# Attention row blocks 4 to 7 copied by ScalarE's DMAs and transposed as fp32r, with two exponentials issued earlier

## The chip, the cores and the metric

The kernel runs on one core of a Trainium2 chip. The metric is the device time of one execution in microseconds, the median over several runs. TensorE (PE) multiplies into PSUM and loads its stationary operand by separate instructions (PEld in the profile); VectorE (DVE), ScalarE (ACT) and GpSimd (POOL) do the element-wise work; DMAs are issued by SyncE (SP) or, as in this change, by ScalarE.

## The reference

One decoder block on x of shape (1024, 1024) in float32: an RMS norm, an input projection, forgetting attention with 8 heads of 64 columns beside a gated mixing path, an output projection with a residual, and a gated MLP with a short causal convolution. The change is in the attention:

```python
c = jnp.cumsum(log_f, axis=1)
...
logits = jnp.einsum('bqhd,bkhd->bhqk', qi, k).astype(jnp.float32) * scale
logits = logits + ci[..., None] - c_k
causal = pi[:, None] >= key_pos[None, :]
logits = jnp.where(causal, logits, -jnp.inf)
p = jax.nn.softmax(logits, axis=-1).astype(v.dtype)
return jnp.einsum('bhqk,bkhd->bqhd', p, v)
```

## The kernel before

Large products run in fp32r, a 4-byte type with a shortened mantissa that TensorE takes in one pass. To keep float32 accuracy each operand is split into a high part (a cast to fp32r) and a low part (the difference, again fp32r), and three products high x high, high x low, low x high are added in PSUM.

**The attention stage** (about 222 to 357 us of the span) works head by head. A head's 1024 query rows are 8 row blocks of 128; block j has (j + 1) x 128 columns because of the causal mask. For each block:

- `logits_mm` (lines 1002 to 1012) multiplies queries and keys into a PSUM tile of `place()`, of which there are two.
- `logits_min` (lines 1014 to 1035) on VectorE writes the masked logits to SBUF, into `places[h, i]`, and takes their row minimum. `places[h, i]` holds the blocks 2i and 2i + 1 side by side; its buffer is chosen by `TTAG`.
- `logits_exp` (lines 1037 to 1040) on ScalarE takes the exponential in place and adds up its rows. Each is followed by a short read of the accumulator.
- `turn_p` (lines 1057 to 1067) transposes 128 x 128 pieces of the finished blocks on TensorE, with the tile itself as the stationary operand and the identity `ident` as the moving one, four pieces to a PSUM bank; ScalarE casts the bank to the high part (line 1065) and VectorE subtracts for the low part (line 1066).
- `values` (lines 1071 to 1090) multiplies the two parts with the head's values.

**The order.** `STEPS` cuts each head into five steps of two groups of transposes (the last step has one). In head h, step s, the loop (lines 1186 to 1262) first issues `turn_p` for the groups of the following step, so the step 4 of head h turns the first two column blocks (k = 0, 1) of head h + 1, from row blocks 4, 5, 6 and 7 in that order. It then runs `values` on what the step before turned, and between the groups the logits and minima of the next head: blocks 7 and 6 in step 0, 5 and 4 in step 1, 3 and 2 in step 2, 1 and 0 in step 3. A minimum goes to the list `due`; the step after takes it over as `last` and issues its exponentials at its end. So exponentials 7 and 6 stand in step 1, 5 and 4 in step 2, 3 and 2 in step 3, 1 and 0 in step 4. TensorE's order is fixed by `seq`; on the other engines instructions are placed by a list scheduler, and `after(tc, later, earlier)` only says that one comes behind the other in the queue. `row_tail` (step 1) writes the row sums to DRAM by a DMA that ScalarE issues (line 963). In heads 0 to 5 products of the gate path (`sg_out`, lines 1104 to 1106) are put in after steps 2 and 4 as filler. The last head has no logits beside it.

Head 0's logits and exponentials come ahead of this loop. The tile tags: `t2` and `t3` have one buffer each, `H` has four, shared by early activations, by `attF` and by blocks 4 to 7 of odd heads.

Of the kernel before, what the change touches and what calls it, by code (L numbers as in the profile page):

```python
# [8 lines left out]
F32 = mybir.dt.float32  # L9
F32R = mybir.dt.float32r  # L10
# [4 lines left out]
P = 128  # L15
# [48 lines left out]
def after(tc, later, earlier):  # L64
    tc.add_manual_dep(later.ins, earlier.ins.name, mybir.DependencyInfo(
        mybir.DependencyClass.NoSync, mybir.DependencyReason.DATA), reason="order")
# [8 lines left out]
def block_kernel(ctx: ExitStack, tc: tile.TileContext, xT, xtok, wuv, wuh, wv0, wva, wvk, wvl, wqk, cpk, bfv,  # L75
                 ggain, g2r, gfr, wsp, woa, wos, wup, wdn, out):
    nc = tc.nc
    act, dve, pool, pe, sp = Line(nc.scalar, tc), Line(nc.vector, tc), Line(nc.gpsimd, tc), nc.tensor, nc.sync

    cst = ctx.enter_context(tc.tile_pool(name="cst", bufs=1))  # L80
# [12 lines left out]
    def nm(s):  # L93
        uid[0] += 1
        return f"{s}_{uid[0]}"

    BUFS = {"x1": 4, "x2": 2, "t3": 1, "t2": 1, "t01": 1, "V": 4, "H": 4, "wy": 2, "gg": 2,
            "pt": 3, "G": 4, "A": 2, "whl": 4, "raw": 4}

    LATE = ("A", "G", "whl", "pt")  # L100
# [1 line left out]
    def sb(tag, shape, dt=F32):  # L102
        return (base if tag == "x1" else raws if tag == "raw" else late if tag in LATE else early).tile(shape, dt, tag=tag, bufs=BUFS[tag], name=nm(tag))

# [27 lines left out]
        pe.matmul(wps, warm[:, 0:P], warm, start=True, stop=True)  # L132
    dve.memset(one, 1.0)
    dve.memset(lim, BIG)
    ident = cst.tile([P, P], F32, name="ident")
    make_identity(nc, ident)
    maskb = cst.tile([P, P], BF16, name="maskb")
    pool.memset(maskb, 0.0)
    pool.affine_select(out=maskb, in_=maskb, pattern=[[-1, P]], compare_op=ALU.is_ge,
# [44 lines left out]
    def xset(tags):  # L184
        r = []
        for t in tags:
            if t == "x1":
                r.append([sb(t, [P, 2, 512], F32R) for _ in range(2)])
            else:
                b = sb(t, [P, 2, 2, 512], F32R)  # L190
                r.append([b[:, 0], b[:, 1]])
        return r

    RAW = {n: [sb(t, [P, 2, 512]) for t in tags] for n, tags in (
        ("x21", ("V", "V")), ("x11", ("H", "H")), ("x22", ("x1", "x2")), ("x12", ("t3", "t2")))}
    XS = {n: xset(tags) for n, tags in (("B11", ("V", "V")), ("T2", ("H", "H")), ("B21", ("x1", "x2")))}

    def xs(n, hl, k):
        return XS[n][k // 2][hl][:, k % 2, :]

    def x2(n, hl, j):
        return XS[n][j][hl]

# [55 lines left out]
    for p_ in range(2):  # L259
        t = sb("G", [P, 2, 2, 512])  # L260
# [37 lines left out]
    for o in (slice(0, 256), slice(256, 512)):  # L298
        h, l, src = xs("B11", 0, 0)[:, o], xs("B11", 1, 0)[:, o], xr("x11", 0)[:, o]
# [86 lines left out]
    for k in range(4):  # L386
        dve.scalar_tensor_tensor(out=xr("x12", k), in0=xr("x12", k), scalar=gk(k), in1=tmp[k // 2][2][:, k % 2],
                                 op0=ALU.mult, op1=ALU.subtract)
    XS["T3"] = xset(("x1", "x2"))
    for j in range(2):  # L390
# [5 lines left out]
    for w in gb:  # L396
        dve.tensor_tensor(out=w[:, 0, :], in0=w[:, 0, :], in1=w[:, 1, :], op=ALU.add)
    XS["T1"], mid = xset(("H", "H")), sb("t3", [P, 4, 512])
    for k in range(4):
# [13 lines left out]
    for k in range(4):  # L413
        t2 = tmp[k // 2][1][:, k % 2]
# [290 lines left out]
    gg = []  # L705
# [53 lines left out]
    V, vhigh = [], []  # L759
# [21 lines left out]
    def seq(m):  # L781

        if order:
            after(tc, m, order[0])
        order[:] = [m]
# [98 lines left out]
    abs_, places = [None] * 8, {}  # L884
# [66 lines left out]
    attF = [None] * 4  # L951


    TTAG = [("gg", "gg"), ("wy", "wy"), ("t2", "H"), ("t3", "H")]
    exs = []
    def row_tail(h):

        p, hh, rs = h // 2, h % 2, rows[h]
# [38 lines left out]
    casts, los = [], []  # L997
# [16 lines left out]
    def logits_min(h, j, ps):  # L1014

        i, jj = j // 2, j % 2
        w1, w2 = (2 * i + 1) * P, (2 * i + 2) * P
        if jj == 1:
            tp = sb(TTAG[i][h % 2], [P, w1 + w2])
            places[h, i] = (tp[:, 0:w1], tp[:, w1:w1 + w2])  # L1020
        n = (j + 1) * P
        mn = sml.tile([P, 1], F32, tag="mn", name=nm("mn"))
        o, s, k = places[h, i][jj], ps[:, 0:n], msk[:, 1024 - n:1024]
        if chunk(n) < min(n, 512):
            o, k = (v.rearrange("p (b c) -> p b c", b=2) for v in (o, k))
            s = ps.rearrange("p (b c) -> p b c", b=2)[:, :, 0:chunk(n)]
        m = dve.tensor_tensor_reduce(out=o, in0=s, in1=k, scale=ss1[:, j:j + 1],
                                     scalar=lim[:, 0:1], op0=ALU.add, op1=ALU.min, accum_out=mn)
        if h and j == 5:
            after(tc, m, recips[h - 1])  # L1030
        if h and j == 3:
            after(tc, m, los[-1])
        if h == 7 and j == 0:
            after(tc, m, los[-2])
        return mn

    def logits_exp(h, j, mn):
        t = places[h, j // 2][j % 2]
# [18 lines left out]
    def turn_p(g):  # L1057

        ptr = bank()
        pt = sb("pt", [P, 2, 512], F32R)  # L1060
        for half, k, j0, c, w in spans(g):
            for j in range(j0, 4 * half + 4):
                o = c + (j - j0) * P
                seq(pe.transpose(ptr[:, o:o + P], places[g[0], j // 2][j % 2][:, k * P:(k + 1) * P], ident))  # L1064
        casts.append(act.copy(pt[:, 0, :], ptr))  # L1065
        los.append(dve.tensor_tensor(out=pt[:, 1, :], in0=ptr, in1=f32(pt[:, 0, :]), op=ALU.subtract))  # L1066
        return pt
# [86 lines left out]
    def fill(key):  # L1154
        for _ in range(FILL.get(key, 0)):
            next(filler, None)
# [27 lines left out]
    due = []  # L1184
    turned = [turn_p(g) for g in STEPS[0]]
    for n, step in enumerate(STEPS):
        h, s = n // 5, n % 5
        if s == 0 and h < 6:
            head_loads(h + 2)
        if h == 7 and s == 0:  # L1190
            for _ in filler:
                pass
            wo_load((0, 1))
            wo_load((2, 3))
        if h in (2, 4, 6) and s == 4:
            for o in (slice(0, 512), slice(512, 1024)):
                pair_half(h // 2 - 1, o)
        now, turned = turned, []
        last, due = due, []
        if n == 35:  # L1200
            psl.release()
            psl = tc.alloc_tile_pool(name="psc", bufs=4, space=bass.MemoryType.PSUM, reuse_waits="tile")
            banks8[0, 0] = lbank()
            wmm(0, 0, banks8[0, 0], (0,))
        for g in STEPS[n + 1] if n + 1 < len(STEPS) else []:
            if n == 36 and turned:
                for e in held + [mrow]:
                    after(tc, logits_exp(*e), casts[-1])
            turned.append(turn_p(g))
            if n == 36 and len(turned) == 2:  # L1210
                after(tc, casts[-1], exs[-1])
        if n == 34:
            mrow = (7, 0, logits_min(7, 0, mrow))
        if n == 33:

            held, last = last, []
        if n == 34:
            last, held = held[:1], held[1:] + last
        if n == 35:
            last, held = held[:1], held[1:]  # L1220
        if s == 1 and h % 2 == 0:
            attF[h // 2] = sb("H", [P, 2, 1024])
        if s == (1 if h < 7 else 2):
            recips[h] = dve.reciprocal(rows[h], rows[h])
        out_copy = None
        if n == 37:
            row_tail(7)
        if n in EARLY:
            wmm(0, 0, banks8[0, 0], EARLY[n])
        if n == 39:  # L1230
            banks8[4, 0] = lbank()
            wmm(4, 0, banks8[4, 0], (0,))
        for c, (g, pt, js) in enumerate(zip(step, now, NEXT[s])):
            out_copy = values(g, pt) or out_copy
            last_copy = out_copy
            if h < 7:
                for j in js:
                    if n == 33 and j == 0:
                        mrow = logits_mm(7, 0, place())
                        continue  # L1240
                    due.append((h + 1, j, logits_min(h + 1, j, logits_mm(h + 1, j, place()))))
            if s == 1 and h < 7 and c == 0:
                row_tail(h)

        for e in last:
            x = logits_exp(*e)
            after(tc, x, casts[-1] if n == 34 else out_copy or casts[-1])
        fill((h, s))
        for _ in range(min(len(SPLIT), 1 if n == 9 else 2)):
            ws_, k, wr = SPLIT.pop(0)  # L1250
            wt = sb("whl", [P, 2, 512], F32R)
            ws_[k] = wt
            after(tc, act.copy(wt[:, 0], wr), out_copy or casts[-1])
            pool.tensor_tensor(out=wt[:, 1], in0=wr, in1=f32(wt[:, 0]), op=ALU.subtract)
        if n == 2:
            vh = sb("A", [P, 2, 4, 256])
            sp.dma_start(out=vh, in_=vu.rearrange("h p m c -> p h m c"))
        if n in UPPER:
            tt = UPPER.index(n)
            low = evac_v(tt, 1, vh[:, tt // 4, tt % 4, :])  # L1260
            after(tc, low(), los[-1])
            after(tc, vhigh[0], exs[-1])
# [186 lines left out]
    for i in range(AHEAD):  # L1449
# [4 lines left out]
        if i == 0:  # L1454

            last = flip(7)
# [219 lines left out]
    for p_, n in ((upl, "B11"), (upl, "T2"), (upl, "B21"), (upl, "T3"), (upr, "T1"), (upr, "T4"), (upr, "B22")):  # L1676
        t = ut_(p_, "x" + n, [P, 2, 4, 512], F32, 1)
# [71 lines left out]
    x1, x3, u2 = ([t[:, m, :] for m in range(4)] for t in big)  # L1749
# [144 lines left out]
```

## Time and profile before

| What | Value |
|---|---|
| Time, median of 3 runs | 1044.55 us (1044.23 to 1044.55) |
| The profiled execution's own time | 1043.81 us |
| Its span (first to last instruction) | 1042.1 us |
| Granted TensorE clock, mean | 0.998 |
| Transposes of the attention, line 1064 | 288, median 272 ns of one |
| Casts of line 1065 | 72, 40.4 us busy, 584 ns |
| Subtractions of line 1066 | 72, 47.4 us busy, 686 ns |

The page counts busy time of each engine. Matmuls are pipelined: one of 272 ns may be followed by the next after less, so what they cost is read from the distance of their starts in the timeline. An entry "x8" in the timeline is a run of eight merged ones, with the time from the first start to the last end. Shapes are written "partitions x elements", `pb<-ident,t` is "written <- read", and a bracket gives the idle time of the engine and what ended it. The waits in the attention stage are few on TensorE; the longest sums belong to engines that are ahead of it:

```profile
ACT pt L1065 <- PE pb L1064: 24.4, 16, 4.6
POOL H L973 <- ACT wy L1039: 23.2, 1, 23.2
DVE pt L1066 <- ACT pt L1065: 10.1, 28, 1.2
```

The columns are who waited for whom, the total in us, the number of waits and the longest.

### The profile page before, as it was taken

Reading aid. Unit: us, or ns where it says so; the run is one execution under the profiler, and the core shown is the slowest. Engines: PE = TensorE matmul, PEld = TensorE weight load, DVE = VectorE, ACT = ScalarE, POOL = GpSimd, SP = SyncE. Lnnn points to the kernel's source line nnn. Section 1 sums busy time; section 2 is a strip of 40 time slices with the busy share of each in tenths; the row PEclk is TensorE's granted clock in tenths of the full one; section 3 lists DMA queues with packets and bytes.
Section 4 is the critical chain, followed back from the end, with each engine's and each line's share of the span. In section 5 each row is a group of like instructions: output and inputs, shape, how many; then the busy total and the mean of one; then the engine's idle time right before and its main releaser. Section 6 shows DMA issues by size and latency. Waiting matters only on the chain.

```text
span 1042.1 us, 14271 instructions
## 1 busy us (share of the span) xinstructions
PE 1034.4 (99%) x4998; PEld 869.6 (83%) x4998; DVE 892.3 (86%) x1302; ACT 564.2 (54%) x1003; POOL 221.9 (21%) x167
## 2 busy tenths in 40 slices
PE   9999999999999999999999999999999999999997
PEld 7988888988888888888888888888888888888886
DVE  6899887888888888998999998898997857997774
ACT  6776632457776857644444444444544544444654
POOL 0000232500322540343334323333331000000000
PEclk9999999999999999999999999999999999999999
DMA  9622558885645553231353432332322998333432
GB/s 340 231 82 97 153 156 250 238 256 171 203 130 172 187 169 111 81 122 60 131 178 131 139 120 71 132 101 81 122 81 91 327 330 293 110 92 101 150 115 99
DMA packets 67467, 161.66 MB, mean 155 GB/s; under 512 B 8110, under 2 KB 9254, under 8 KB 67396
## 3 DMA queue, kind: packets, MB, share of 16 engines
q1 hardware_dynamic: 67124, 160.72, 47.6%
q8 instruction: 39, 0.64, 0.3%
q14 instruction: 32, 0.26, 0.1%
q10 hardware_dynamic: 272, 0.04, 0.0%
HBM read 115.68 MB, written 45.05 MB: 154 GB/s over the span
## 4 chain that ended last, share of the span: by engine, by line
PE 98%; DVE 0%; DMA 0%; ACT 0%; SPq 0%; issue 0%; DVEq 0%
PE pb L1440 23%; PE pk L1440 17%; PE pb L1704 11%; PE pk L1704 9%; PE ps L283 5%; PE pb L283 5%; PE pk L1145 4%; PE pb L1080 3%; PE pb L1064 3%; PE qc L522 2%; PE qd L522 2%; PE qa L522 2%; PE pl L1010 2%; PE ps L873 2%; PE pl L1011 2%; PE pf L1104 1%
## 5 line engine op out<-in xcount | busy, mean ns | idle before, releaser
L1440 PE MATMUL pb<-xT,whb 128*128 128x512 f32 x804 | 189.4, 389 | 0.0
L1440 PEld LDWEIGHTS pb<-xT,whb 128*128 128x128 f32 x804 | 150.9, 188 | 31.4
L1440 PE MATMUL pk<-xB,x 128*128 128x512 f32 x528 | 127.2, 390 | 0.0
L1704 PE MATMUL pb<-whb,x 128*128 128x512 f32 (+1 forms) x528 | 119.2, 387 | 0.0
L1440 PEld LDWEIGHTS pk<-xB,x 128*128 128x128 f32 x528 | 98.8, 188 | 20.8 <-DVE x L172 0.4
L1704 PEld LDWEIGHTS pb<-whb,x 128*128 128x128 f32 x528 | 98.3, 188 | 20.3 <-DVE x L172 0.2
L166 ACT CAST x<-sg 128x512 fp32r<-128x512 f32 x77 | 47.8, 622 | 96.8 <-PE pk L1704 46.1
L166 ACT CAST whb<-sg 128x512 fp32r<-128x512 f32 x82 | 50.5, 617 | 83.9 <-PE pb L1440 83.0
L1704 PE MATMUL pk<-whb,x 128*128 128x512 f32 (+1 forms) x408 | 91.8, 386 | 0.0
L1704 PEld LDWEIGHTS pk<-whb,x 128*128 128x128 f32 x408 | 75.9, 188 | 15.5
L172 DVE TENSOR_TENSOR x<-sg,x 128x512 fp32r<-128x512 f32 x77 | 52.7, 687 | 39.4 <-ACT x L166 39.3
L1490 DVE SCALAR_TENSOR_TENSOR ca<-h,cp,ca 128x1023 f32<-128x1023 f32 (+1 forms) x44 | 67.9, 1544 | 3.9 <-ACT ca L1489 3.9
L1490 DVE SCALAR_TENSOR_TENSOR cg<-h,cp,cg 128x1023 f32<-128x1023 f32 (+1 forms) x44 | 65.5, 1489 | 5.5 <-ACT cg L1489 5.2
L1440 PE MATMUL pb<-xB,whb 128*128 128x512 f32 x264 | 63.8, 389 | 0.0
L1440 PE MATMUL pk<-xT,whb 128*128 128x512 f32 x252 | 61.0, 389 | 0.0
L172 DVE TENSOR_TENSOR whb<-sg,whb 128x512 fp32r<-128x512 f32 x82 | 57.1, 697 | 4.4 <-ACT whb L166 4.3
L1065 ACT CAST pt<-pb 128x512 fp32r<-128x512 f32 x72 | 40.4, 584 | 37.1 <-PE pb L1064 24.4
L1440 PEld LDWEIGHTS pb<-xB,whb 128*128 128x128 f32 x264 | 49.5, 188 | 10.7 <-issue 0.4
L1337 POOL TENSOR_TENSOR sg<-raw 128x512 f32<-128x512 f32 x20 | 30.2, 1511 | 131.1 <-DVE whb L172 74.5
L1066 DVE TENSOR_TENSOR pt<-pb,pt 128x512 fp32r<-128x512 f32 x72 | 47.4, 686 | 10.8 <-ACT pt L1065 10.1
L1440 PEld LDWEIGHTS pk<-xT,whb 128*128 128x128 f32 x252 | 47.2, 188 | 10.0 <-DVE whb L172 0.3
L1080 PE MATMUL pb<-pt,V 128*128 128x512 f32 (+3 forms) x192 | 49.0, 360 | 0.1
(414 smaller groups left out, 2154.1 us busy)
## 6 DMA issues: line engine op xcount, KB each, us to landing
raw<-wup SPq DMA_DIRECT2D x44, 512.0 KB
sg<-hx SPq DMA_DIRECT2D x77, 256.0 KB
hx<-hs SPq DMA_DIRECT2D x44, 256.0 KB
hx<-ca SPq DMA_DIRECT2D x35, 256.0 KB
xT<-wdn SPq DMA_DIRECT2D x28, 256.0 KB
x<-kd SPq DMA_DIRECT2D x24, 256.0 KB
A<-xtok SPq DMA_DIRECT2D x8, 512.0 KB
raw<-wqk SPq DMA_DIRECT2D x8, 512.0 KB
```

Of the source, the lines that this page charges most:

```text
L166: cast[:] = [act.copy(h, src)]
L172: return eng.tensor_tensor(out=l, in0=src, in1=f32(h), op=ALU.subtract)
L283: pe.matmul(banks[m], xs(n, xi, k)[:, ms], w[:, wi, :], start=(first and k == 0 and c == 0 and (own or m % 2 == 0)), stop=(k == 3 and c == ...
L522: pe.matmul(ps, w[:, wi, ks], xs(n, xi, k), start=(first and c == 0), stop=(c == 11), skip_group_check=True)
L1064: seq(pe.transpose(ptr[:, o:o + P], places[g[0], j // 2][j % 2][:, k * P:(k + 1) * P], ident))
L1065: casts.append(act.copy(pt[:, 0, :], ptr))
L1066: los.append(dve.tensor_tensor(out=pt[:, 1, :], in0=ptr, in1=f32(pt[:, 0, :]), op=ALU.subtract))
L1080: seq(pe.matmul(po[half][:, o:o + w], lhs, pt[:, s, c:c + w], start=(new and s == 0), stop=(s == 1 and (half, k) in ((1, 6), (0, 3))), ski ...
L1145: seq(pe.matmul(ps, attT[k][:, a, ts_], w[:, b, :], start=(k == 0 and n == 0), stop=(k == 3 and n == 2)))
L1440: pe.matmul(ps, w[:, wi, ks], xb[:, xi, k, :], start=(first and n == 0), stop=(n == 11), skip_group_check=True)
L1490: return [dve.scalar_tensor_tensor(out=c[:, n:1024], in0=h[:, 0:1024 - n], scalar=w[2 - n], in1=c[:, n:1024], op0=ALU.mult, op1=ALU.add) f ...
L1704: pe.matmul((banks[bk + m] if ps is None else ps)[:, o], xh[:, xi, ms], wh[:, wi, o], start=((first and p_ == 0 or new) and n == 0), stop= ...
```

## The change

It has four parts.

1. The identity is made in a scratch tile and copied by ScalarE to an fp32r tile `identr`; `ident` is the same tile read as float32.
2. Heads 1 to 7 keep the exponentials of blocks 4 to 7 in `t2` and `t3`, one buffer each. In step 2 of head h, `copy_p` has ScalarE issue DMAs that copy head h + 1's blocks 7 and 6 to a tile `C3`, behind the step's casts, and at the end of the step its blocks 5 and 4 to `C2`, behind the step's last exponential. Head 0 keeps its blocks in `C2` and `C3` directly and is not copied.
3. `turn_p` reads blocks 4 to 7 of heads 1 to 7 from the copies, as fp32r, with `identr` as the moving operand, and writes PSUM as fp32r. Blocks 0 to 3, and head 0, are transposed as before. Of a head's 36 transposes 26 read blocks 4 to 7.
4. In steps 0 and 1 the first of the two minima just taken is passed on at once: exponential 7 is issued at the end of step 0 and exponentials 6 and 5 at the end of step 1, which leaves 4 for step 2.

```diff
-    BUFS = {"x1": 4, "x2": 2, "t3": 1, "t2": 1, "t01": 1, "V": 4, "H": 4, "wy": 2, "gg": 2,
+    BUFS = {"x1": 4, "x2": 2, "t3": 1, "t2": 1, "t01": 1, "V": 4, "H": 2, "C2": 1, "C3": 1, "wy": 2, "gg": 2,
...
-    ident = cst.tile([P, P], F32, name="ident")
-    make_identity(nc, ident)
+    identr = cst.tile([P, P], F32R, name="ident")
+    ident = identr.bitcast(F32)
+    id0 = sb("t01", [P, P])
+    make_identity(nc, id0)
+    act.copy(identr, id0)
...
-    XS = {n: xset(tags) for n, tags in (("B11", ("V", "V")), ("T2", ("H", "H")), ("B21", ("x1", "x2")))}
+    XS = {n: xset(tags) for n, tags in (("B11", ("V", "V")), ("T2", ("C2", "C3")), ("B21", ("x1", "x2")))}
...
-    TTAG = [("gg", "gg"), ("wy", "wy"), ("t2", "H"), ("t3", "H")]
-    exs = []
+    TTAG = ("gg", "wy", "t2", "t3")
+    CTAG = (None, None, "C2", "C3")
+    exs, turns = [], {}
...
-            tp = sb(TTAG[i][h % 2], [P, w1 + w2])
+            tp = sb(CTAG[i] if h == 0 and CTAG[i] else TTAG[i], [P, w1 + w2])
             places[h, i] = (tp[:, 0:w1], tp[:, w1:w1 + w2])
+            turns[h, i] = places[h, i]
...
+    def copy_p(h, i, behind_):
+
+        w1, w2 = (2 * i + 1) * P, (2 * i + 2) * P
+        tp = sb(CTAG[i], [P, w1 + w2])
+        turns[h, i] = (tp[:, 0:w1], tp[:, w1:w1 + w2])
+        for jj in (1, 0):
+            x = act.dma_start(out=turns[h, i][jj], in_=places[h, i][jj])
+            after(tc, x, behind_)
+
...
-                seq(pe.transpose(ptr[:, o:o + P], places[g[0], j // 2][j % 2][:, k * P:(k + 1) * P], ident))
+                t, o_ = turns[g[0], j // 2][j % 2][:, k * P:(k + 1) * P], ptr[:, o:o + P]
+                if g[0] and CTAG[j // 2]:
+                    seq(pe.transpose(o_.bitcast(F32R), t.bitcast(F32R), identr))
+                else:
+                    seq(pe.transpose(o_, t, ident))
...
+        if s == 2 and h < 7:
+            copy_p(h + 1, 3, casts[-1])
...
+        if s < 2 and h < 7:
+            last.append(due.pop(0))
         for e in last:
             x = logits_exp(*e)
             after(tc, x, casts[-1] if n == 34 else out_copy or casts[-1])
+        if s == 2 and h < 7:
+            copy_p(h + 1, 2, exs[-1])
```

## The prediction

> **What bounds the kernel now.** I read the page first: engines, then the chain that ended last.
>
> ```profile
> span 1042.1 us, 14271 instructions
> PE 1034.4 (99%) x4998; PEld 869.6 (83%) x4998; DVE 892.3 (86%) x1302; ACT 564.2 (54%) x1003; POOL 221.9 (21%) x167
> ...
> PE 98%; DVE 0%; DMA 0%; ACT 0%; SPq 0%; issue 0%; DVEq 0%
> ```
>
> TensorE is the chain: 98% of it. So time taken from TensorE counts, as long as nothing else becomes late. The second view cuts the attention stage into head periods (a row runs from the first transposes of one head to those of the next; the last one shows the beginning of head 7).
>
> ```profile
> core 0: us, PE busy (x) PEld busy (x) DVE busy (x) ACT busy (x) POOL busy (x), PEclk, DMA share, GB/s
> 240.00:258.20 18.20, 18.20 (x112) 16.09 (x112) 16.53 (x35) 14.02 (x33) 0.00 (x0) 1.00 0.53 161
> 258.20:276.30 18.10, 18.10 (x111) 16.04 (x110) 15.63 (x32) 15.00 (x35) 11.48 (x10) 1.00 0.63 189
> 312.60:330.80 18.20, 18.20 (x113) 16.13 (x111) 15.04 (x31) 12.43 (x29) 0.00 (x0) 1.00 0.65 190
> 330.80:346.50 15.70, 15.68 (x100) 13.93 (x99) 14.37 (x30) 12.32 (x29) 14.57 (x17) 1.00 0.38 136
> 345.53:353.00 7.47, 7.47 (x48) 6.64 (x49) 6.57 (x15) 6.77 (x19) 7.12 (x8) 1.00 0.48 152
> ```
>
> PE is busy in every microsecond of a full head period (18.2 us). VectorE has 1.7 to 3.2 us to spare per period, ScalarE 3.1 to 5.8 us, the DMA engines a third to a half of their time. Only head 6's period (330.80 on, with no gate products left as filler) is short, 15.7 us.
>
> **The change, part by part.** *The transposes.* Each head has 36 of them: 10 read row blocks 0 to 3, 26 read blocks 4 to 7. In heads 1 to 7 those 26 become fp32r, 182 in all. The views by line and by form, and the timelines of PE and PEld, give the prices:
>
> ```profile
> L1064 PEld LDWEIGHTS pb<-ident,t x104: 137/140/144, 221.9 to 341.7; 128*128 128x128 f32 x104
> L1064 PE MATMUL pb<-ident,t x104: 270/272/297, 222.0 to 341.8; 128*128 128x128 f32 x104
> 330.79 1.06 PE L1064 MATMUL pb<-ident,t 128*128 128x128 f32 x8
> 276.15 0.22 PE L1010 MATMUL pl<-x,x 128*128 128x128 f32 x1
> 276.21 0.28 PE L1011 MATMUL pl<-x,x 128*128 128x128 f32 x1
> 276.29 0.20 PEld L1064 LDWEIGHTS pb<-ident,H 128*128 128x128 f32 x2
> 271.32 0.19 PEld L1010 LDWEIGHTS pl<-x,x 128*128 128x128 f32 x1
> 271.43 0.19 PEld L1011 LDWEIGHTS pl<-x,x 128*128 128x128 f32 x1
> L817 PEld LDWEIGHTS pb<-G,pt 128*128 128x128 f32 x28 | 5.2, 190 | 0.7
> L817 PE MATMUL pb<-G,pt 128*128 128x256 f32 x28 | 6.4, 379 | 0.0
> L873 PE MATMUL ps<-whl,H 128*128 128x256 f32 x96 | 11.7, 283 | 0.0
> ```
>
> (The views write f32 for fp32r operands too; L817 multiplies plain fp32, L873, L1010 and L1011 fp32r.) Eight transposes take 1.06 us, the last 0.27 of which is its own latency, so one follows the other after (1.06 - 0.27)/7 = 0.11 us. An fp32r product of the same 128 columns is followed after 0.06 (276.15 to 276.21). That is the lower bound of an fp32r transpose. The upper bound is today's 0.11: two fp32r weight loads that have only short products to hide behind stand 0.11 apart (271.32 and 271.43), and each transpose has a weight load of its own. So the gain is 0 to 0.05 us on each of 182, that is 0 to 8.9 us.
>
> I take 0.06, for two reasons. What streams through twice as slowly is the type: 256 plain fp32 columns take 379 - 283 = 96 ns longer than 256 fp32r columns, nearly the 107 that would double the streaming. And what makes a weight load short is that it belongs to a transpose, not its type: plain fp32 loads take 190 ns like fp32r ones, but a transpose's 140, and the first two of a run are started within 0.06 of each other (two of 0.14 in 0.20). So I expect an fp32r transpose to have the short load and the short stream.
>
> The Trainium skill speaks against it: its page "TensorE: Matmul & The Clock Gate", section "LDWEIGHTS (loading the stationary operand)", gives a load as columns/1.2 ns, 107 ns for 128 columns. The fp32r loads 0.11 apart agree with it; the two transpose loads 0.06 apart do not. By that rule the transposes would gain nothing, which is the first rival below.
>
> By place, 0.049 us each: head h+1's first 8 are turned in step 4 of head h (0.39 us), 8 in its own step 0, 8 in step 1, 2 in step 2 (0.10): 1.27 us per head. A head period would shrink from 18.2 to 16.9 us, still above VectorE's 16.5 and ScalarE's 15.0.
>
> *The copies.* Four DMAs a head, 28 in all, of 512, 448, 384 and 320 KB, SBUF to SBUF, which this trace does not show. Blocks 7 and 6 go after step 2's casts and are wanted two steps later, two fifths of 18.2 us; they are hidden, at the price of the copies below if that did not do. Blocks 5 and 4 go after exponential 4, and block 4 is the first that step 4 turns. The room, from the end of exponential 4 to that turn:
>
> ```profile
> 272.61 0.81 ACT L1039 ACTIVATE H<-H,mn 128x640 f32<-128x640 f32 x1
> 276.33 1.06 PE L1064 MATMUL pb<-ident,H 128*128 128x128 f32 x8
> 323.49 0.24 ACT L962 COPY t<-pb 8x128 f32<-8x128 f32 x1
> 323.64 1.04 ACT L1039 ACTIVATE t<-t,mn 128x896 f32<-128x896 f32 x1
> 323.76 0.27 ACTq L963 DMA_DIRECT2D rsd<-t  x1
> 325.62 0.93 ACT L1039 ACTIVATE t<-t,mn 128x768 f32<-128x768 f32 x1
> 326.55 0.81 ACT L1039 ACTIVATE t<-t,mn 128x640 f32<-128x640 f32 x1
> 329.65 0.59 ACT L1065 CAST pt<-pb 128x512 fp32r<-128x512 f32 x1 [2.19 <-PE pb L1064]
> 344.72 0.81 ACT L1039 ACTIVATE H<-H,mn 128x640 f32<-128x640 f32 x1
> 346.48 1.06 PE L1064 MATMUL pb<-ident,H 128*128 128x128 f32 x8
> 0.81 0.41 ACTq L120 DMA_DIRECT2D g<-cpk  x1
> 3.27 0.51 ACT L55 ACTIVATE V<-H,g 128x256 fp32r<-128x256 f32 x1 [0.52 <-DMA g<-cpk]
> 1.26 0.42 SPq L240 DMA_DIRECT2D raw<-wuv  x1
> 3.85 0.43 DVE L55 CAST wy<-raw 128x512 fp32r<-128x512 f32 x1 [0.97 <-DMA raw<-wuv]
> ```
>
> The room is 330.79 - 327.36 = 3.4 us in head 5 (heads 0, 3 and 4 are like it), 276.33 - 273.42 = 2.9 in head 2 (head 1 is like it), and 346.48 - 345.53 = 0.95 in head 6. Since TensorE gains 0.88 us from step 0 to step 4 while ScalarE's chain of casts and exponentials, full from step 1 on, only begins about 0.4 to 0.5 sooner, the room shrinks by some 0.4: to 3.0, 2.5 and 0.55. A DMA from issue to the first use of its data took 2.5 us for 4 KB issued by ScalarE (0.81 to 3.27) and 2.6 for 256 KB (1.26 to 3.85). For 320 KB behind 384 KB that start 0.8 us sooner I estimate 2.8 us after exponential 4; bounds 2.4 (no queueing) and 4.5 (the 704 KB at head 5's 190 GB/s, 3.8, and some share lost to SyncE's traffic). So four heads just fit, heads 1 and 2 wait 0.3 each. In head 6 exponential 5 no longer stands just ahead of exponential 4, which may end some 0.9 us sooner; there I take a wait of 1.4 us, and it has no cover. By the Trainium skill ("DMA: Bandwidth & Descriptors", section "Issuing engines are not separate DMA queues") DMAs from ScalarE and SyncE share the same 16 engines, so the ScalarE queue buys no bandwidth; the 0.65 busy share speaks for little queueing, and the estimate stands.
>
> Behind block 4's waiting DMA in ScalarE's order stands the cast of step 3, before which ScalarE idles 2.19 us: nobody waits. Issuing costs 0.27 us each (L963), and is hidden under the running ACTIVATE as that one is (323.76 inside 323.64 to 324.68); uncovered it is 1.1 us per head against ScalarE's 3.1 idle.
>
> *Exponentials 7 and 5 sooner.* The same work in another order. Cost nothing while the casts and the low halves behind them still come before PE's next logits; see the third rival. *identity as fp32r:* one short copy in ScalarE's idle 0.52 us ahead of 3.27 (0.24 us for 128 columns, estimated from L962's 8x128 copy); nothing. *Buffers:* the copies' two tiles replace two of H; every earlier reader is done steps before. Nothing.
>
> *Sum.* Heads 1 to 6: 6 x 1.27 = 7.6. Less 0.6 (heads 1, 2) and 1.4 (head 6). Head 7's own 1.27: I keep 0.3, because ScalarE is busy for 6.77 of the 7.47 us from 345.53 on and its casts set the pace there. 7.6 - 2.0 + 0.3 = 5.9 us. The profiled execution took 1043.81 us (span 1042.1 and 1.7 around it): 1037.9. The median of the runs shown is 0.74 above it, 1044.55: **1038.7 us**. About 0.2% (2.1 us) is what a measurement can tell from no change.
>
> **Rivals.** (1) *The weight load binds*: fp32r loads keep 0.11 apart and the transposes run as now. For it: every fp32r load here. Against it: the transposes' 140 ns. Only the first of each run of eight is quicker (0.05 x 21 = 1.0), and head 6's wait of about 1 remains: 1044.5. This is also "the change doesn't do what it says". Chance 0.17.
>
> (2) *Slower: the copies land late.* One mechanism, at step 4 of each head: the first transpose waits for block 4's copy. With L from exponential 4's end to landing, the waits are 4 x (L - 3.0) + 2 x (L - 2.5) + (L - 1.4); they eat the 7.9 at about L = 3.8 and make the kernel measurably slower above L = 4.05. At the bound of 4.5 they are 6 + 4 + 3.1 = 13.1: 1049.8. For it: 1.7 MB more per head beside 2.9 to 3.5 MB, and no SBUF-to-SBUF row. Against it: 2.6 us for 256 KB. Chance 0.18.
>
> (3) *The exponentials displace the casts.* In head 5, minimum 7 is ready within 0.05 us of the cast it now competes with:
>
> ```profile
> 319.60 1.33 DVE L1027 CUSTOM_DVE_ANT_0 t<-pl,t,lim 128x1024 f32<-128x1024 f32 x1
> 320.97 0.59 ACT L1065 CAST pt<-pb 128x512 fp32r<-128x512 f32 x1 [2.01 <-DVE mn L1027]
> 322.35 1.16 ACT L1039 ACTIVATE t<-t,mn 128x1024 f32<-128x1024 f32 x1
> 324.19 0.94 DVE L1027 CUSTOM_DVE_ANT_0 t<-pl,t,lim 128x640 f32<-128x640 f32 x1
> 324.86 0.40 PE L1010 MATMUL pl<-x,x 128*128 128x512 f32 x1
> ```
>
> If the exponential (1.16 us) goes first, the low halves and minimum 5 on VectorE come up to 0.9 us later; PE's logits 3 at 324.86 need minimum 5's PSUM tile, free at 324.19, so 0.6 of it is covered now and 0.1 after the gain. About 0.7 x 6 = 4.2 lost: 1042.9. Chance 0.12.
>
> **How the numbers follow.** Forecast 1038.7, chance 0.53 (its own range 1036 to 1041.5). Faster: 0.51 of the forecast, 0.02 of rival 2 (L under 3.5), 0.04 of rival 3: 0.57. Within 0.2%: 0.02 + 0.13 of rival 1 + 0.02 + 0.05: 0.22. Slower: 0.04 of rival 1 + 0.14 of rival 2 + 0.03 of rival 3: 0.21. The range reaches down to all 8.9 us kept (1035.6) and up to rival 2 with L about 4.1 (1047), leaving out the later landings.
>
> **What would show it.** Runs of eight fp32r transposes of about 0.70 us rather than 1.06 show the first step right; 1.0 shows rival 1. Head periods near 17 us show the gain kept; PEld or PE waiting for a copy ahead of step 4's transposes, in head 6 about 1.4 us and elsewhere under 0.4, shows or refutes the landing; a PE wait for a minimum ahead of logits 3 shows rival 3. The prediction is wrong if block 4's copy lands later than 3.8 us after its exponential, or if an fp32r transpose keeps the 0.11.

## The result, and the profile after

The changed kernel takes **1080.21 us** (median of 4 runs, 1079.96 to 1084.4) where the kernel before took 1044.55 beside it: a ratio of 1.0351, 95% interval 1.0326 to 1.0376. The forecast was 1038.7 with a range to 1047. The kernel is 36 us slower, not 6 us faster, and the range does not hold it.

From the page of the profiled execution after (1080.09 us), the engines, the queue of ScalarE's DMAs (packets, MB, share of 16 engines) and the chain:

```profile
span 1078.3 us, 14326 instructions
...
PE 1040.1 (96%) x4998; PEld 873.0 (81%) x4998; DVE 894.2 (83%) x1302; ACT 564.3 (52%) x1004; POOL 220.8 (20%) x167
...
q10 hardware_dynamic: 4304, 11.97, 3.1%
...
PE 64%; DMA 2%; DVE 1%; POOL 1%; issue 1%; ACT 1%; ACTq 0%
```

TensorE's busy share of the span fell from 99% to 96%. The chain can't be set against the 98% of before: it is followed back only to about 326 us of the span, and its shares add up to 70%. The 11.97 MB are the 28 copies (7 x 1.70 MB) and small transfers that were there before. The head periods, from the first transposes of one head to those of the next, in the windows view:

```profile
core 0: us, PE busy (x) PEld busy (x) DVE busy (x) ACT busy (x) POOL busy (x), PEclk, DMA share, GB/s
221.56:247.07 25.51, 18.05 (x108) 15.64 (x107) 15.90 (x34) 11.89 (x27) 0.00 (x0) 0.92 0.92 271
247.07:270.02 22.95, 20.61 (x110) 17.88 (x110) 16.96 (x35) 14.48 (x33) 0.00 (x0) 0.86 0.54 167
270.02:291.95 21.93, 19.35 (x110) 16.89 (x110) 16.01 (x32) 14.87 (x33) 11.69 (x10) 0.92 0.80 233
291.95:311.71 19.76, 17.79 (x109) 15.61 (x110) 16.05 (x32) 13.17 (x30) 0.01 (x1) 1.00 0.77 231
353.32:380.46 27.14, 15.36 (x98) 13.42 (x98) 14.16 (x27) 11.15 (x24) 20.30 (x22) 0.86 0.58 199
```

PE's busy time is no longer the length of its row. Before, these periods were 18.0 to 18.2 us and head 6's 15.7; the seven together took 124.5 us, now 158.9. So 34.4 of the 36.2 us of the spans lie here, most of all in heads 0 (25.5) and 6 (27.1). PE idles until this (waits view of PE, 222 to 400 us; who waited for whom, total us, times, longest):

```profile
PE pb L1081 <- DMA C<-t: 25.6, 5, 11.1
PE pb L1081 <- DVE H L1108: 4.3, 2, 2.3
```

L1081 is the fp32r transpose, `C<-t` the copy, L1108 VectorE's addition to a head's output. The landing ends all seven waits, also the two that the view puts down to L1108: in each head PE goes on 0.13 to 0.14 us after block 4's copy has landed. One head in detail, first ScalarE's timeline (start, duration; ACTq issues DMAs), then PE's:

```profile
282.77 0.92 ACT L1054 ACTIVATE t<-t,mn 128x768 f32<-128x768 f32 x1
283.49 0.47 ACTq L1049 DMA_DIRECT2D C<-t  x1
284.35 0.48 ACTq L1049 DMA_DIRECT2D C<-t  x1
284.98 0.76 ACTq L1049 DMA_DIRECT2D C<-t  x1
285.15 0.83 ACT L1054 ACTIVATE t<-t,mn 128x640 f32<-128x640 f32 x1
286.10 0.90 ACTq L1049 DMA_DIRECT2D C<-t  x1
```

```profile
289.10 0.27 PE L1016 MATMUL pl<-x,x 128*128 128x128 f32 x1
291.95 0.84 PE L1081 MATMUL pb<-ident,C 128*128 128x128 f32 x8 [2.58 <-DMA C<-t]
292.63 0.75 PE L1099 MATMUL pb<-pt,V 128*128 128x384 f32 x4
```

The copies of blocks 7, 6, 5 and 4 are issued at 283.49, 284.35, 284.98 and 286.10: within 2.6 us, not two steps apart. The first two could not have gone much sooner here, because `C3` has one buffer and the transposes of step 2 read it until 282.31. The trace's packet records show them as one burst of 1664 KB from 285.25 to 291.35, in that order, so block 4, which PE turns first, lands last, at 291.81. That is 5.8 us after its exponential ended at 285.98; in heads 1 to 5 it is 5.3 to 6.1 us, in heads 0 and 6 11.0 and 11.1. The DMA view of 285 to 292 us says what the burst takes:

```profile
q10 hardware_dynamic: 576, 1.70, 68.2%
q1 hardware_dynamic: 370, 0.79, 35.4%
```

The packets of these 1.70 MB took 0.682 x 7 = 4.8 us of the 16 engines' time. With SyncE's own traffic (q1) the two shares add up to over 100%, so the engines had no time to spare. In head 0 SyncE moved more still: 2.72 MB beside 1.71 MB on ScalarE's queue from 233 to 248 us.

**The theory** after this reading: PE waits for block 4's copy, because the copies of 7 and 6 are in front of it on the same engines. Against it stood that ScalarE loses the time for the issues, that the reordered exponentials cost it, or that the fp32r transposes themselves do.

### The profile page after: what moved, and what is told of

It reads as the page before. It is cut to its first block, busy times and chain, and to the rows that moved or that the text cites. A ratio compares the mean times of both kernels' runs of the same rounds, so it can differ in the third digit from the quotient of the medians.

```text
span 1078.3 us, 14326 instructions
## 1 busy us (share of the span) xinstructions
PE 1040.1 (96%) x4998; PEld 873.0 (81%) x4998; DVE 894.2 (83%) x1302; ACT 564.3 (52%) x1004; POOL 220.8 (20%) x167
## 3 DMA queue, kind: packets, MB, share of 16 engines
q10 hardware_dynamic: 4304, 11.97, 3.1%
## 4 chain that ended last, share of the span: by engine, by line
PE 64%; DMA 2%; DVE 1%; POOL 1%; issue 1%; ACT 1%; ACTq 0%
PE pb L1465 22%; PE pk L1465 16%; PE pb L1729 11%; PE pk L1729 8%; PE pk L1164 4%; DMA C<-t 2%; PE pb L1099 1%; PE pb L1415 1%; DMA raw<-wup 1%; PE pb L1081 1%; PE pb L1164 1%; POOL whl L1156 0%; DVE cg L1515 0%; POOL whl L1155 0%; ACT pt L1084 0%
## 5 line engine op out<-in xcount | busy, mean ns | idle before, releaser
L1729 PEld LDWEIGHTS pb<-whb,x 128*128 128x128 f32 x528 | 98.3, 188 | 20.3 <-DVE x L175 0.2
L1465 PEld LDWEIGHTS pb<-xB,whb 128*128 128x128 f32 x264 | 49.5, 188 | 10.8 <-issue 0.5
L1099 PE MATMUL pb<-pt,V 128*128 128x512 f32 (+3 forms) x192 | 51.5, 376 | 0.1
```

The lines of the kernel that those rows point to most:

```text
L1099: seq(pe.matmul(po[half][:, o:o + w], lhs, pt[:, s, c:c + w], start=(new and s == 0), stop=(s == 1 and (half, k) in ((1, 6), (0, 3))), ski ...
L1465: pe.matmul(ps, w[:, wi, ks], xb[:, xi, k, :], start=(first and n == 0), stop=(n == 11), skip_group_check=True)
L1729: pe.matmul((banks[bk + m] if ps is None else ps)[:, o], xh[:, xi, ms], wh[:, wi, o], start=((first and p_ == 0 or new) and n == 0), stop= ...
```

## The experiments

Times are medians; the ratio is to the kernel before on the same chip, with its 95% interval. The table gives the head periods of each kernel (heads 0 to 6, us; distances of the first transposes in its trace), which decide more than the totals.

| Kernel | us | ratio | 0 | 1 | 2 | 3 | 4 | 5 | 6 |
|---|---|---|---|---|---|---|---|---|---|
| before | 1044.55 | | 18.0 | 18.2 | 18.2 | 18.1 | 18.2 | 18.2 | 15.7 |
| after | 1080.21 | 1.0326 to 1.0376 | 25.5 | 23.0 | 21.9 | 19.8 | 20.1 | 21.5 | 27.1 |
| 1 exponentials only | 1045.01 | 0.9991 to 1.0010 | 18.0 | 18.2 | 18.2 | 18.2 | 18.2 | 18.2 | 16.2 |
| 2 fp32r, no copies | 1042.11 | 0.9963 to 0.9984 | 18.0 | 17.8 | 17.7 | 18.2 | 17.7 | 17.6 | 15.2 |
| 3 copies, fp32 turns | 1084.01 | 1.0363 to 1.0409 | 26.3 | 22.6 | 21.1 | 20.4 | 20.3 | 19.9 | 26.4 |
| 4 copies unread | 1059.82 | 1.0127 to 1.0157 | 18.0 | 19.2 | 19.6 | 19.3 | 19.3 | 19.2 | 17.3 |
| 5 blocks 7, 6 only | 1053.36 | 1.0055 to 1.0096 | 18.0 | 18.1 | 19.4 | 19.0 | 18.7 | 18.3 | 16.5 |
| 6 blocks 5, 4 only | 1058.03 | 1.0080 to 1.0142 | 21.0 | 19.5 | 20.3 | 17.9 | 17.8 | 17.8 | 21.4 |
| 7 head 7 not copied | 1069.46 | 1.0196 to 1.0268 | 22.5 | 23.1 | 22.0 | 19.7 | 19.9 | 21.3 | 15.8 |
| 8 issued by SyncE | 1078.25 | 1.0287 to 1.0346 | 21.5 | 21.3 | 21.8 | 18.6 | 19.3 | 18.6 | 32.3 |
| 9 unread, order kept | 1054.91 | 1.0076 to 1.0106 | 18.0 | 18.2 | 18.2 | 18.2 | 18.2 | 18.2 | 16.2 |
| 10 after, order kept | 1076.52 | 1.0276 to 1.0321 | 25.5 | 22.1 | 20.7 | 20.5 | 20.1 | 19.6 | 26.7 |
| 11 7, 6, order kept | 1051.19 | 1.0040 to 1.0073 | 18.0 | 18.6 | 18.4 | 18.5 | 17.9 | 18.2 | 15.9 |
| 12 fp32r, no low half | 1034.40 | 0.9882 to 0.9911 | 18.0 | 16.1 | 16.2 | 16.1 | 16.1 | 16.1 | 14.5 |

### 1. The exponentials alone

```diff
+        if s < 2 and h < 7:
+            last.append(due.pop(0))
         for e in last:
             x = logits_exp(*e)
```

> The kernel before with the fourth part of the change alone: the exponentials of blocks 7 and 5 half a step sooner, no copies, fp32 transposes. Theory (the copies land late and TensorE waits for them): this part costs nothing by itself, 1043 to 1046 us. Rival (the reordered exponentials displace the casts): a good part of the 36 us is here, 1055 us or more.

No difference in the time. The periods of heads 0 to 5 are as before, and head 6's is 16.2 us instead of 15.7. The rival of the reordered exponentials is out.

### 2. The fp32r transposes alone

```diff
+    o = t.bitcast(F32R) if h and j > 3 else t
-    exs.append(act.activation(t, t, AF.Exp, bias=mn, scale=-1.0, accum_out=rows[h][:, j:j + 1]))
+    exs.append(act.activation(o, t, AF.Exp, bias=mn, scale=-1.0, accum_out=rows[h][:, j:j + 1]))
...
-                seq(pe.transpose(ptr[:, o:o + P], places[g[0], j // 2][j % 2][:, k * P:(k + 1) * P], ident))
+                t, o_ = places[g[0], j // 2][j % 2][:, k * P:(k + 1) * P], ptr[:, o:o + P]
+                if g[0] and j > 3:
+                    seq(pe.transpose(o_.bitcast(F32R), t.bitcast(F32R), identr))
```

(The minima are written as fp32r in the same way.)

> The kernel before with the fp32r identity and fp32r transposes of blocks 4 to 7 of heads 1 to 7, without any copy: the minima and the exponentials of these blocks are written as fp32r (rounded) in place instead, and the transposes read them directly. Theory: what the transposes gain stands 0.024 us apart per transpose in the trace of after (0.085 against 0.109), over 182 of them 4.4 us: 1039 to 1041 us. By the prediction's own step (0.06 apart) 1035.6 us. Rival (the fp32r weight load of 0.14 us sets the pace and the turned blocks gain nothing or lose): 1044.5 us or more.

The gain is 2.7 us (1044.83 against 1042.11), less than the theory's 4.4 and far less than the prediction's 8.9. Its PE timeline:

```profile
298.88 0.80 PE L1070 MATMUL pb<-ident,t 128*128 128x128 f32 x8
299.52 0.70 PE L1088 MATMUL pb<-pt,V 128*128 128x512 f32 x2
```

The last transpose's own latency is 0.25 here, so they follow each other after (0.80 - 0.25)/7 = 0.08 us (the median distance of two starts is 0.084), not 0.06. And the matmul behind the run starts 0.086 us after the last transpose, where the median behind an fp32 transpose was 0.028: what the run saves is partly given back at its end. From first transpose to that matmul 0.64 us pass here, 0.68 in the changed kernel (291.95 to 292.63), and 0.82 before, from the 330.79 that the prediction shows to this (the medians are 0.63, 0.64 and 0.79):

```profile
331.61 0.77 PE L1080 MATMUL pb<-pt,V 128*128 128x384 f32 x4
```

### 3. The copies, turned as fp32

```diff
-                if g[0] and CTAG[j // 2]:
-                    seq(pe.transpose(o_.bitcast(F32R), t.bitcast(F32R), identr))
-                else:
-                    seq(pe.transpose(o_, t, ident))
+                seq(pe.transpose(o_, t, ident))
```

> The changed kernel with all its copies, and TensorE turning from the copies, but as fp32 as before. Theory: the whole loss stays and the 4.4 us of the fp32r transposes are given back, most of them: 1081 to 1086 us. Rival (the fp32r transposes or their weight loads are what costs): well under 1080 us, towards 1045.

The whole loss stays: it comes with the copies, not with the type of the transposes.

### 4 and 9. Copies that nobody reads

In run 4 the same 28 copies go to a scratch in DRAM, issued at the same places; the transposes read the originals.

```diff
+            x = act.dma_start(out=cpd[2 * i + jj - 4, :, 0:n], in_=places[h, i][jj])
+            after(tc, x, behind_)
```

> The kernel before with the sooner exponentials and with the same 28 copies issued by ScalarE at the same places, but to a scratch in DRAM that nobody reads; the transposes read the originals as fp32. Theory (the loss is TensorE's wait for the landing): nearly all of the 36 us goes, 1044 to 1049 us. Rival (ScalarE is held up by issuing, 0.5 to 2.3 us for each DMA, so casts and exponentials come late whoever reads the copies): 1065 us or more. Rival (the DMA engines are shared with SyncE's loads, which come late): between, with waits on loads in the rows of TensorE.

1059.82: 20 us less than after, and 24 less than run 3, which also turns as fp32. So most of the loss is the waiting, as the theory has it, but 15 us stayed that it did not explain. (The copies go to DRAM here and the buffers are those of before, so more than the reading differs; runs 5, 6 and 10 show the waits without that.) In heads 1 to 5 some 1.1 us a head stayed. PE's waits from 222 to 345 us, and VectorE's timeline in one head:

```profile
PE pb L1072 <- DVE pt L1074: 5.5, 6, 1.2
```

```profile
297.84 0.54 DVE L1028 CUSTOM_DVE_ANT_0 gg<-pl,t,lim 128x256 f32<-128x256 f32 x1 [0.46 <-PE pl L1012]
...
298.58 0.41 DVE L1028 CUSTOM_DVE_ANT_0 gg<-pl,t,lim 128x128 f32<-128x128 f32 x1 [0.19 <-PE pl L1012]
...
298.92 0.69 DVE L1074 TENSOR_TENSOR pt<-pb,pt 128x512 fp32r<-128x512 f32 x1
```

VectorE takes the minima of blocks 1 and 0 (256 and 128 columns) first and the low half of L1074 after them; in the kernel before the low half and the addition to the output (L1089) come first:

```profile
294.67 0.68 DVE L1089 TENSOR_TENSOR H<-pb,H 64x512 f32<-64x512 f32 x1
295.38 0.54 DVE L1027 CUSTOM_DVE_ANT_0 gg<-pl,t,lim 128x256 f32<-128x256 f32 x1
```

The planner that places the instructions put them in another order, and the copies are all that run 4 has more than run 1, whose order is the old one. The order of the changed kernel differs in the same way. Run 9 is run 4 with one edge that restores it, and nothing else:

```diff
-        if h and j == 3:
+        if h and j in (1, 3):
             after(tc, m, los[-1])
```

> The kernel with the copies that nobody reads, with one ordering edge more on VectorE: the minimum of block 1 stands behind the low half of the step, as it stood in the kernel before. With the copies in the program the planner had put the minima of blocks 1 and 0 ahead of that low half and of the addition to the head's output. Order theory (the 1.1 us a head that unread copies cost are this new order, in which a PSUM bank comes free late): the periods of heads 1 to 5 return to 18.2 us, in all 1053 to 1056 us; what stays is head 6. Rival (it is ScalarE's time for issuing the copies): no change, 1058 to 1062 us.

```profile
296.35 0.69 DVE L1074 TENSOR_TENSOR pt<-pb,pt 128x512 fp32r<-128x512 f32 x1 [0.36 <-ACT pt L1073]
297.07 0.68 DVE L1097 TENSOR_TENSOR H<-pb,H 64x512 f32<-64x512 f32 x1
297.79 0.54 DVE L1028 CUSTOM_DVE_ANT_0 gg<-pl,t,lim 128x256 f32<-128x256 f32 x1
```

The periods of heads 1 to 5 are 18.16 us again, to the hundredth, with ScalarE issuing 1.66 MB of copies in each. So in these heads the issues of copies that nobody reads cost nothing, and the order did. What stayed, 10 us, is at the passage to head 7. ScalarE's timeline of run 9 there, and SyncE's:

```profile
350.15 4.60 ACTq L1042 DMA_DIRECT2D cpd<-H  x2
354.80 0.59 ACT L1073 CAST pt<-pb 128x512 fp32r<-128x512 f32 x1 [6.85 <-DMA cpd<-H]
```

```profile
347.86 0.33 SPq L1287 DMA_DIRECT2D raw<-wup  x1
```

The fourth copy is issued at 354.43, though its block was ready before 348, and ScalarE's next cast stands behind it for 6.85 us. In the trace every DMA reports its landing on a numbered semaphore: the fourth copy and the load of 347.86 have the same number, the load landed at 354.33, and the issue began 0.10 us later; the instruction just ahead of it in ScalarE's queue is a wait for that number. The third copy stands in the same way to the wup load before that one (landed 350.07, issued 350.15), and in the trace of after the last three copies of head 6 stand so to three of SyncE's loads, within 0.08 us each. So ScalarE, and all its casts and exponentials, waits for weights that SyncE loads for the next stage. No run changed the numbers alone; run 7 takes head 7's copies away.

### 5, 6 and 11. Half of the copies

Blocks that are not copied keep two alternating buffers, as before. The edit of run 5:

```diff
-    TTAG = ("gg", "wy", "t2", "t3")
-    CTAG = (None, None, "C2", "C3")
+    TTAG = (("gg", "gg"), ("wy", "wy"), ("t2", "H"), ("t3", "t3"))
+    CTAG = (None, None, None, "C3")
...
-        if s == 2 and h < 7:
-            copy_p(h + 1, 2, exs[-1])
```

> The changed kernel with blocks 7 and 6 alone copied and turned as fp32r (15 of the 26 transposes of a head, 960 KB instead of 1664 KB); blocks 5 and 4 are turned from their own buffers as before. Three things are to be weighed: TensorE's wait for the landing, ScalarE's time for the issues (the copies that nobody read cost 1.1 us a head), and ScalarE's stand in head 6, where an issue waits for an earlier load with the same completion semaphore. Landing theory: at about 280 GB/s 960 KB land some 3.5 us after the first issue, ahead of TensorE's need, so heads 1 to 5 wait for nothing; 2.5 us gained by the transposes, some 3 us lost on ScalarE, some us in heads 0 and 6: 1045 to 1051 us. If the size of the burst does not matter: 1060 us or more.

And of run 6:

```diff
-    TTAG = ("gg", "wy", "t2", "t3")
-    CTAG = (None, None, "C2", "C3")
+    TTAG = (("gg", "gg"), ("wy", "wy"), ("t2", "t2"), ("t3", "H"))
+    CTAG = (None, None, "C2", None)
...
-        if s == 2 and h < 7:
-            copy_p(h + 1, 3, casts[-1])
```

`turn_p` reads a copy and turns it as fp32r where `CTAG` names a tile, so in each run the other two blocks are turned as fp32.

> The changed kernel with blocks 5 and 4 alone copied and turned as fp32r (11 of 26 transposes, 704 KB); blocks 7 and 6 as before. This is the prediction's own case, in which the copies of 7 and 6 cost nothing: by its step the landing comes 2.8 us after the exponential of block 4, and the waits are 2 us in all: 1043 us. By the landing theory, with 704 KB alone on the queue: 3 to 4 us after the exponential, so waits of up to 1 us a head, and head 6 as in after: 1048 to 1056 us. If block 4's copy is late whatever stands ahead of it on its queue: 1065 us or more.

Run 6 is the case that the prediction had worked out. ScalarE and PE in head 3:

```profile
297.00 0.83 ACT L1054 ACTIVATE t<-t,mn 128x640 f32<-128x640 f32 x1
...
297.94 0.47 ACTq L1049 DMA_DIRECT2D C<-t  x1
```

```profile
301.12 0.28 PE L1016 MATMUL pl<-x,x 128*128 128x128 f32 x1
301.23 0.33 PE L1081 MATMUL pb<-ident,C 128*128 128x128 f32 x2
```

Block 4's copy landed at 300.56, 2.7 us after the exponential's end at 297.82. PE goes on from 301.12 to 301.23 without a wait, and heads 3 to 5 take 17.8 to 17.9 us, less than before. The 2.8 us of the prediction came out for 704 KB with little beside them (in head 4, also 2.8 us, SyncE moved 0.26 MB from 314 to 319 us), if with block 5's copy issued 1.8 us ahead of block 4's and not 0.8. In heads 0, 2 and 6 the landing took 6.6, 4.8 and 7.2 us, beside loads of SyncE; in head 2 (DMA view of 276 to 284 us) these are the larger part:

```profile
q1 hardware_dynamic: 616, 1.34, 58.4%
q10 hardware_dynamic: 288, 0.72, 32.2%
```

The whole, 1058.03, is above the 1048 to 1056 expected: three heads met such loads and not two, and head 1, whose copy lands after 2.9 us, runs at a granted clock of 0.91 behind head 0's wait (PE busy in all of its 19.5 us).

Run 5 lost 8.4 us (1053.36 against 1044.93), more than expected too: PE waits for copies in five places, 4.3 us in all, and VectorE's order is changed again from head 1 on, in heads 3 to 5 by less. Run 11 is run 5 with the edge of run 9:

> Blocks 7 and 6 alone copied, with the ordering edge. Order theory: heads 2 to 5, at 18.3 to 19.4 us without the edge, come to 17.9 us: 1048 to 1051 us. Landing theory alone (960 KB late in these heads): no change, 1052 to 1055 us.

Heads 2 to 5 came from 18.8 to 18.25 us in the mean, not to 17.9. The total is 2.2 us lower, but its interval overlaps run 5's, so the time alone does not decide. Its waits from 222 to 385 us:

```profile
PE pb L1081 <- DMA C<-t: 4.6, 4, 3.3
```

3.3 us of these are at head 7; the other 1.3 are about what keeps four heads from 17.9. Even the smaller burst is late in places.

### 7. Head 7 not copied

```diff
-        if s == 2 and h < 7:
+        if s == 2 and h < 6:
             copy_p(h + 1, 3, casts[-1])
```

(The same for blocks 5 and 4; head 7 is turned as fp32.)

> The changed kernel without the four copies of head 7 (made in head 6); head 7's blocks are turned as fp32 from their own buffers. After lost 9 to 11 us in that one period, 27.1 us against 17 to 18. Theory (ScalarE stands in front of the copies' issues until the loads of the next stage with the same completion semaphores land, and with it the exponentials): all of that goes, less 0.6 us for slower transposes: 1069 to 1073 us. If the loss of head 6 comes from the loads that contend for the DMA engines with whatever else moves: 1076 us or more.

As expected, 1069.46. Head 6's period is 15.8 us again: all of its 11.3 us hung on these four copies.

### 8. Issued by SyncE

```diff
-            x = act.dma_start(out=turns[h, i][jj], in_=places[h, i][jj])
+            x = sp.dma_start(out=turns[h, i][jj], in_=places[h, i][jj])
```

> The changed kernel with the 28 copies issued by SyncE instead of ScalarE. Rival (ScalarE's time for issuing and its stands are a large part): 1060 to 1070 us, casts and exponentials back where they were. Landing theory (TensorE waits because 1.66 MB in one burst come late): 1073 to 1085 us, the wait for the landing still of 2 us or more in each head; and SyncE, held by each copy's wait for its exponential, starts the loads behind it later.

1078.25, not to be told from after. Two things work against each other. Heads 1 to 5 gain 6.6 us together (their periods sum up to 99.6 against 106.25), and head 0 gains 4.0. The planner also keeps VectorE's old order in this kernel, but against run 10, which keeps it too, heads 1 to 5 are still 3.3 us shorter: block 4's copy lands 4.1 to 5.6 us after its exponential, in run 10 5.5 to 6.1. So the queue that issues was not free of cost for copies that are read; whether it is ScalarE's issue times or the changed place of SyncE's loads is not separated. In head 6 the copies stand in SyncE's queue behind the weights, and PE waits 16.3 us. SyncE's timeline, and PE's waits up to 370 us and up to 385 us:

```profile
361.42 3.88 SPq L1351 DMA_DIRECT2D raw<-wup  x2
365.35 0.48 SPq L969 DMA_DIRECT2D H<-rsd  x1
365.92 4.15 SPq L1049 DMA_DIRECT2D C<-t  x4
```

```profile
PE pb L1081 <- DMA C<-t: 7.6, 3, 3.3
...
PE pb L1081 <- DMA C<-t: 23.9, 4, 16.3
```

### 10. The changed kernel with VectorE's order kept

```diff
-        if h and j == 3:
+        if h and j in (1, 3):
             after(tc, m, los[-1])
```

> The changed kernel with the same ordering edge, nothing else. If the waits for the landing stand alone and cover whatever the order on VectorE costs: 1079 to 1083 us. If the order delays the banks, with them the exponentials and the copies behind them, it is part of the loss in heads 1 to 5: 1072 to 1077 us, with waits for the landing of 1 to 1.5 us a head left there and the long ones of heads 0 and 6 unchanged.

1076.52: the order is worth 3.7 us here. Every wait in the view is for a copy, one in each of seven heads:

```profile
PE pb L1081 <- DMA C<-t: 30.2, 7, 10.8
```

The waits are as long as in the changed kernel, though. The windows view of all seven periods together (before, run 2, after and run 10, columns as above) shows where the 3.7 us went:

```profile
221.98:346.48 124.50, 124.39 (x750) 109.88 (x749) 107.03 (x216) 90.11 (x203) 32.38 (x32) 1.00 0.58 175
223.12:345.30 122.18, 121.90 (x750) 106.32 (x749) 106.84 (x216) 89.97 (x203) 32.03 (x32) 1.00 0.60 178
221.56:380.46 158.90, 128.21 (x750) 111.92 (x749) 109.50 (x219) 90.33 (x203) 38.61 (x38) 0.92 0.74 224
223.14:378.31 155.17, 124.12 (x750) 108.44 (x749) 109.29 (x219) 90.40 (x203) 38.41 (x38) 0.95 0.76 229
```

PE is idle for 158.90 - 128.21 = 30.7 us in the changed kernel and for 31.1 in run 10. The difference is in its busy time, at a granted clock of 0.92 against 0.95. The same matmuls take 121.9 us in run 2 at 1.00, so the lower clock goes with 6.3 us in the changed kernel and 2.2 in run 10. How the order brings about the lower clock is not shown.

### 12. A version that beats both

Run 2 leaves a low half that is zero wherever the exponentials are already fp32r. Run 12 does not compute it and does not multiply with it:

```diff
+            n_ = 1 if h and half else 2
-            for s in range(2):
+            for s in range(n_):
```

(VectorE's subtraction is cut to the columns of blocks 0 to 3.) It changes the arithmetic: logits and exponentials of blocks 4 to 7 of heads 1 to 7 are rounded to fp32r, as in run 2.

> The kernel without copies whose exponentials of blocks 4 to 7 are written as fp32r, heads 1 to 7, and in which the low halves of these blocks, which are then zero, are neither computed by VectorE nor multiplied with the values by TensorE. TensorE is busy through the whole stage, so its time should go: per head eight matmuls of 512, 512, 512, 512, 512, 384, 256 and 128 columns at about 0.23 us per 512, 1.5 us, for 7 heads 10 us: 1030 to 1034 us. Rival (VectorE or ScalarE becomes the bound when TensorE is this much shorter): 1036 to 1042 us.

**1034.40 us**, a ratio of 0.9896 (0.9882 to 0.9911), 0.4 us above the range expected. The windows view of one period:

```profile
257.10:273.20 16.10, 16.10 (x102) 14.16 (x102) 11.86 (x26) 14.88 (x34) 11.50 (x10) 1.00 0.77 213
```

A period is 16.1 us, PE is busy in all of it and still the bound.

## Why the prediction was wrong, step by step

- **"Blocks 7 and 6 ... are hidden"** failed, and this is the step that decided. "Two steps later" is true of when they are wanted, but not of when they go: the copies of 7 and 4 are issued 2.6 us apart and move as one burst. The landing was then counted for 704 KB where 1664 KB go in order. Measured: 5.3 to 6.1 us after the exponential in heads 1 to 5 and 11 in heads 0 and 6 rather than 2.8, so the sign that the prediction had named, a landing later than 3.8, came in every head; with 704 KB alone it is 2.7 (run 6, head 3). The prediction's own waits with L = 5.8 would be 4 x 2.8 + 2 x 3.3 + 4.4 = 22 us: rival 2 had the mechanism, and its upper end of 4.5 us was too low because it summed the same 704 KB.
- **The busy share of 0.65 "speaks for little queueing"** failed. It is a mean over the period. A head's loads and copies come in bunches: head 0's period has a share of 0.92, and in run 6 the landing of the same 704 KB takes 2.7 us in head 3 and 6.6 to 7.2 in heads 0 and 6. The Trainium skill's rule ("DMA: Bandwidth & Descriptors", section "Issuing engines are not separate DMA queues") that DMAs run on the same 16 engines whichever engine starts them agrees with run 8, where the copies from SyncE's queue still keep PE waiting for up to 3.3 us in heads 0 to 5.
- **The transposes**: right in direction, 3 to 4 times too large. 0.08 us apart instead of 0.06 and 0.06 us given back behind a run; 2.7 us in all instead of 8.9. The lower bound came from one pair of products and did not hold for a run of eight transposes, each with a load of its own. The Trainium skill has a figure for that stream, about 81 ns for a pair of load and matmul at 128 columns ("TensorE: Matmul & The Clock Gate", section "Back-to-back issue gap"); the 84 or 85 ns here agree with it, and by it the gain would have been estimated at 182 x (0.109 - 0.081) = 5 us. Rival 1 (no gain) was wrong too.
- **The issues, "hidden" on ScalarE**: right in heads 1 to 5 for copies that nobody reads (run 9), although each takes 0.47 to 2.27 us in the changed kernel and not 0.27; for copies that are read up to 3.3 us stay open (run 8). Wrong in head 6, where the question was not how long an issue takes but what it waits for: 6.85 us behind a load of another queue.
- **VectorE's order was in no step.** That the planner would reorder it around new DMAs was not thought of. It cost 4.9 us in run 4, as waits for a PSUM bank, and 3.7 in the changed kernel (run 10), as time at a lower clock.
- **Exponentials sooner, 0**: right (run 1). Rival 3 is out. Identity and buffers, nothing: no run shows anything of them; in run 2 the identity is part of a gain.
- **Head 6, a wait of 1.4 us**: 11.1 measured (10.8 in run 10). This was the place marked as having no cover, and it is the largest single loss, but by the stand of ScalarE's issues and by the contending loads, which the estimate left out.

In sum, of the 35.7 us 34.4 lie in the seven periods. PE's added idle time is 30.6 of them, nearly all of it the seven waits for copies (29.9; 7.3 at the end of head 0, 11.1 at the end of head 6). The other 3.8 are busy time: 6.3 us with the lower clock, among them the 3.7 of VectorE's order, less 2.5 for the transposes (124.39 against 121.90). The prediction's sum had no term for the clock. The rest, about 1.3 us, lies behind the seventh period and is not separated by a run.

## What to carry to other kernels

A transfer that is "early" is only out of the way if it is issued early, and for that the buffer that it writes must be free by then: list the issue times of everything on the same DMA engines, and count all bytes ahead of the one that is waited for. Where a new DMA enters a queue of an engine that also computes, look for what its issue can wait for (a landing elsewhere), and after a planner has run compare the order of every engine with the order before, since an engine that the change does not touch may have moved. If a copy exists only to give data another type, writing that type in the first place is the cheaper experiment.

## What the runs showed of the hardware

- An fp32r transpose of 128 x 128 is followed by the next after 0.085 us (fp32: 0.109), and by the next product after 0.086 (fp32: 0.028); its own latency is 0.25 against 0.27.
- SBUF-to-SBUF copies of 1.70 MB took 4.8 us of the 16 DMA engines' time and 6.1 us from first to last packet (280 GB/s) beside SyncE's loads. Issuing one from ScalarE took 0.47 us at least (run 6: 0.47 to 0.53, with two a head) and up to 2.27 in the changed kernel, with four close together; the one of 4 KB in the same queue took 0.27.
- The granted clock was 1.00 in the period that ends with a wait of 2 us, 0.92 in that which ends with 7, 0.86 in the one behind it and in the one that ends with 11. The 110 matmuls of the period at 0.86 kept PE busy for 20.6 us, the 109 of the one at 1.00 for 17.8.
